# A hybrid attention, retention and MLP layer on one core: the MLP's weight sums move to the retention and through DRAM, and its blocks become one stream of loads

## The chip, the core and the metric

The kernel is one launch on one core of a Trainium2 chip. The metric is device time in microseconds; a kernel's time is the median of its runs. All arithmetic is float32. A matrix product is made in three TensorE passes over a high and a low part of each operand (type fp32r): high times high, high times low, low times high. The high part is a cast by ScalarE, the low part a subtraction by VectorE; together they are called a split here. TensorE is PE in the profile (PEld its weight loads), VectorE DVE, ScalarE ACT, GpSimd POOL, and SyncE SP; SP's queue issues every DMA.

## The reference

One layer over 1024 tokens of width 1024 with 256 context tokens. Cut to what matters here:

```python
# retention, 4 heads, chunks of 128 tokens, in two directions
out   = einsum(scores, vc) + einsum(qc, state) * xi
state = g_chunk * state + einsum(kc * zeta, vc)
...
x = x + g1 * _merge(o_na, o_ret, xga, xgb, w_proj_na[l], w_proj_ret[l], w_out[l])
hx2 = _modulate(_rmsnorm(x, norm2_g[l]), sh2, sc2)
x = x + g2 * _conv_ffn(hx2, w_up[l], conv_w[l], conv_b[l], w_down[l])

def _conv_ffn(h, w_up, conv_w, conv_b, w_down):
    u = h @ w_up                      # 1024 x 1024 by 1024 x 5632
    ...                               # depthwise convolution over 3 tokens
    a, val = jnp.split(u, 2, axis=-1)
    return (jax.nn.silu(a) * val) @ w_down   # 1024 x 2816 by 2816 x 1024
```

## The kernel before

The stages follow one another: modulation and first products, neighbourhood attention, retention, gates and projections, the output projection, then the MLP as an up product, a convolution and a down product. A planner in the framework sets the order of the instructions on every engine from the recorded program and its own costs; only the very end is written out by hand (`tc.manual_schedule()`). Each engine then works its list strictly in that order, and so does SP's queue: a transfer that waits for an engine holds back every transfer behind it.

**The MLP** makes its products by Strassen's scheme in Winograd's form: seven block products in place of eight, each of sums of blocks. With blocks A11, A12, A21, A22 the sums are S1 = A21 + A22, S2 = S1 - A11, S3 = A11 - A21, S4 = A12 - S2; on the other side T1 to T4 in the same way. There are 22 column blocks j of the up product (`NF`), in pairs of `NH` = 11. The first two are made plainly (`PLAIN`), the other 20 by `Unit7`. `Unit7.load` (L1544 to L1550) loads four 128x512 blocks of `w_up` and lets GpSimd make the four sums `s`; `prod` splits a block or a sum into `wc` and multiplies (L1590). Then `conv` makes a block of the activation; for the second block of a pair GpSimd makes the activation's own four sums `sa` (L1519), and all seven go to DRAM as `d_a`.

**The down product** has seven steps of 11 blocks (`steps`). For each block it loads an activation block from `d_a` (`ra`, split into `ahl`) and takes a weight block or a sum (split into `wc`), and makes 12 matmuls on four banks `y`. GpSimd makes the sums of `w_down` (`sub`, L1676) after the first and the second step in the program's order: for T1 the blocks come as `ur`, the sum is stored to DRAM as `d_w` (L1684) and loaded again for the fifth step; T2, T3 and T4 stay in SBUF tiles `T`.

**The retention** has four heads. A head's work comes in 14 slots: 10 of `front` (two chunks of context, eight of tokens: project a chunk to queries, keys and values) and four of `gate`. `slot` runs a slot's main work in three steps; between them it puts `turn` (the transposes `tp` of the chunk before), `mix` (the chunk outputs of the head before) and `state` (`kz`, `dS`). GpSimd has three small jobs there, each awaited by others: `r` (L1110), the end of the rotary embedding, from which PE makes `tp` and ScalarE and VectorE make `kz`; `SS` (L1170), the low part of the states, from which PE makes `Q`; and `mvr` (L1197), a power. The head's weights come as `raw<-in_w_ret` and `raw<-in_w_rg` in three buffers (L86).

Of the kernel before, what the change touches and what calls it, by code (L numbers as in the profile page):

```python
# [16 lines left out]
P = 128  # L17
D = 1024
KB = D // P
T = 1024  # L20
# [20 lines left out]
def tile_hybrid_layer(ctx, tc: tile.TileContext, io, dbg=None):  # L41
# [18 lines left out]
    d_w = dram.tile([NF // 2, P, 512], F32, name="d_w")  # L60
# [1169 lines left out]

    def slot(main, mix, head=None, i=None):
        def step():
            next(main, None)

# [45 lines left out]
    for _ in tl:  # L1280
        pass
# [201 lines left out]
    NH = NF // 2  # L1483
    A11, A12, A22, S1, S2, S3, S4 = range(7)

    def ur_tile(name):
        return rp.tile([P, 512], F32, tag="r", bufs=12, name=name)

    def ur_load(src, name="ur"):
        t = ur_tile(name)  # L1490
        sync.dma_start(t, src)
        return t

# [30 lines left out]
    def comb(c):  # L1524
        t = [tpl.tile([P, 4, KH, P], F32R, name=f"T{c}{i}") for i in range(2)]
        for b in range(4):
            raw = ur_load(d_t[c, b], "b")
            split(t[0][:, b], t[1][:, b], raw.rearrange("p (k t) -> p k t", k=KH))
# [11 lines left out]
    class Unit7:  # L1540
# [3 lines left out]
        def load(self):  # L1544
            self.a21, self.a22, self.a11, self.a12 = [ur_load(io["w_up"][self.j, b, i], "a") for b, i in ((1, 0), (1, 1), (0, 0), (0, 1))]
            self.s1, self.s2, self.s3, self.s4 = (ur_tile("s") for _ in range(4))
            pool.tensor_tensor(self.s1, self.a21, self.a22, ALU.add)
            pool.tensor_tensor(self.s2, self.s1, self.a11, ALU.subtract)
            pool.tensor_tensor(self.s3, self.a11, self.a21, ALU.subtract)
            pool.tensor_tensor(self.s4, self.a12, self.s2, ALU.subtract)  # L1550

        def prod(self, bank, a, c, first, last):
            w = wtile()
            split(w[:, 0], w[:, 1], a)
# [3 lines left out]
        def step(self, n):  # L1558
            if n == 0:
                self.load()  # L1560
# [5 lines left out]
                self.prod(self.X, self.a11, "B11", True, False)  # L1566
                act.copy(self.p1, self.X)  # L1567
            elif n == 1:
                self.prod(self.Y, self.s2, "T2", True, False)
                vec.tensor_tensor(self.u2, self.Y, self.p1, ALU.add)  # L1570
            elif n == 2:
                self.prod(self.Z, self.s1, "T1", True, False)
            elif n == 3:
                self.prod(self.Y, self.s3, "T3", False, False)
                vec.tensor_tensor(self.u3, self.Y, self.p1, ALU.add)  # L1575
                vec.tensor_tensor(self.value[:, 512:1024], self.Z, self.u3, ALU.add)
            elif n == 4:
                self.prod(self.X, self.a12, "B21", False, True)
                act.copy(self.gate[:, 0:512], self.X)
            elif n == 5:  # L1580
                self.prod(self.Y, self.a22, "T4", False, True)
                vec.tensor_tensor(self.value[:, 0:512], self.Y, self.p1, ALU.add)
            else:
                self.prod(self.Z, self.s4, "B22", False, True)
# [7 lines left out]
    seq = [j + NH * i for j in range(NH) for i in range(2)]  # L1592

    PLAIN = 2
# [11 lines left out]
    for _, i, n in sorted((7 * i + 2 * n, i, n) for i in range(PLAIN, NF) for n in range(7)):  # L1606
# [16 lines left out]
    wd = io["w_down"]  # L1623
# [235 lines left out]
```

## Time and profile before

| | us |
|---|---|
| runs | 1840.24, 1847.33, 1847.97; median 1847.33 |
| the profiled execution | 1837.61 |
| its span, first to last instruction | 1835.8 |
| PE busy in the span | 1758.8 |
| attention | 90 to 395 of the span |
| retention | 395 to 790 |
| gates and projections | 790 to 1040 |
| output projection | 1040 to 1157 |
| up product and convolution | 1157 to 1575 |
| down product | 1575 to the end |

The profile names a group by line, engine, operation and tiles (out<-in, buffer numbers left out). "Idle before" is the time in which the engine had nothing to run ahead of that group, and the arrow names what ended most of it. In a list of waits the last three fields are the total in us, the number of waits and the longest. Matmuls overlap: one of 128x512 is shown at some 390 ns, but one starts every 230 ns or so. A few matmul records are missing from the trace.

### The profile page before, as it was taken

The numbers are of one execution on the slowest core, as the hardware profiler recorded it, in microseconds if no ns is written. First come the engines' busy times: TensorE is split into PE (matmuls) and PEld (weight loads), VectorE is DVE, ScalarE is ACT, GpSimd is POOL, SyncE is SP. The second block draws the span as 40 slices with busy tenths as digits, with TensorE's granted clock in tenths as the row PEclk, the third lists the DMA queues.
The fourth block names the chain that finished last, engine by engine and source line by source line (L and its number), as shares of the span: only waits on it lengthen the run. The fifth ranks groups of instructions, "written<-read, shape, count | busy, mean of one in ns | idle before, by whom it ended". The sixth has DMA issues, their size and how long they took to land.

```text
span 1835.8 us, 24501 instructions
## 1 busy us (share of the span) xinstructions
PE 1758.8 (96%) x8477; PEld 1452.0 (79%) x8477; DVE 1217.0 (66%) x2386; ACT 824.0 (45%) x1768; POOL 517.7 (28%) x445
## 2 busy tenths in 40 slices
PE   8799999999999999999999999999999999938997
PEld 4588888888888888888888788788888888737886
DVE  5878887665666665631354657778888888635756
ACT  5666666553434342423422234544444444323544
POOL 2600000001212122210003400445554554356434
PEclk9799999999999999999999999999999999969999
DMA  9134344321212030323442435523323234688733
GB/s 353 46 112 133 95 121 144 117 83 35 69 33 81 17 99 16 92 86 111 148 127 62 137 138 187 190 75 121 109 89 113 87 102 134 233 308 275 251 119 145
DMA packets 121694, 229.10 MB, mean 125 GB/s; under 512 B 13888, under 2 KB 26336, under 8 KB 121568
## 3 DMA queue, kind: packets, MB, share of 16 engines
q1 hardware_dynamic: 121568, 227.52, 38.1%
q8 instruction: 67, 1.10, 0.3%
q14 instruction: 59, 0.48, 0.1%
HBM read 176.59 MB, written 48.25 MB: 122 GB/s over the span
## 4 chain that ended last, share of the span: by engine, by line
PE 76%; DMA 6%; POOL 5%; issue 5%; DVE 4%; ACT 2%; SPq 1%; POOLq 0%; ACTq 0%; DVEq 0%
PE u L1590 21%; PE mm L107 5%; PE mm L109 5%; PE mm L108 5%; PE mm L120 4%; PE mm L118 4%; PE mm L119 4%; DMA ur<-in_w_down 2%; PE R L506 2%; PE g L107 2%; PE g L108 2%; PE g L109 2%; PE om L118 2%; PE om L120 2%; PE ptp L488 2%
## 5 line engine op out<-in xcount | busy, mean ns | idle before, releaser
L1590 PE MATMUL y<-wc,ahl 128*128 128x512 f32 x924 | 215.7, 395 | 38.2 <-ACT ahl L81 31.3
L1590 PEld LDWEIGHTS y<-wc,ahl 128*128 128x128 f32 x924 | 175.9, 191 | 77.7 <-ACT ahl L81 31.7
L1590 PE MATMUL u<-T,wc 128*128 128x512 f32 x960 | 232.1, 396 | 3.4 <-ACT pu L1567 3.4
L1590 PEld LDWEIGHTS u<-T,wc 128*128 128x128 f32 x960 | 180.5, 188 | 48.4 <-ACT pu L1567 4.3
L108 PE MATMUL mm<-low,wc 128*128 128x512 f32 (+1 forms) x456 | 173.7, 381 | 0.0
L107 PE MATMUL mm<-hx,wc 128*128 128x512 f32 x392 | 158.1, 403 | 0.3 <-DVE vc L216 0.3
L109 PE MATMUL mm<-hx,wc 128*128 128x512 f32 x392 | 155.4, 396 | 0.0
L82 DVE TENSOR_TENSOR wc<-raw,wc 128x512 fp32r<-128x512 f32 x140 | 103.8, 745 | 55.1 <-ACT wc L81 54.7
L81 ACT CAST wc<-raw 128x512 fp32r<-128x512 f32 x140 | 86.8, 621 | 61.9 <-DMA raw<-in_w_gate 14.0
L1590 PE MATMUL u<-h2a,wc 128*128 128x512 f32 x480 | 112.8, 390 | 0.2 <-DVE pu L1575 0.2
L1590 PEld LDWEIGHTS u<-h2a,wc 128*128 128x128 f32 x480 | 90.0, 188 | 20.0 <-DVE pu L1575 0.6
L108 PEld LDWEIGHTS mm<-low,wc 128*128 128x128 f32 x456 | 86.0, 189 | 11.5
L81 ACT CAST wc<-s 128x512 fp32r<-128x512 f32 x80 | 49.6, 621 | 98.6 <-PE u L1590 91.6
L120 PE MATMUL mm<-wc,low 128*128 128x512 f32 (+1 forms) x240 | 91.5, 381 | 0.0
L109 PEld LDWEIGHTS mm<-hx,wc 128*128 128x128 f32 x392 | 73.7, 188 | 14.0
L82 DVE TENSOR_TENSOR wc<-s,wc 128x512 fp32r<-128x512 f32 x80 | 81.5, 1021 | 3.8 <-ACT wc L81 3.5
L107 PEld LDWEIGHTS mm<-hx,wc 128*128 128x128 f32 x392 | 73.9, 188 | 12.0 <-PE c L120 0.7
L82 DVE TENSOR_TENSOR ahl<-ra,ahl 128x512 fp32r<-128x512 f32 x77 | 65.3, 856 | 23.2 <-ACT ahl L81 23.2
L1325 POOL TENSOR_TENSOR col<-col,bcol 128x32 f32<-128x32 f32 x1 | 0.3, 256 | 282.3 <-DVE aw L533 282.3
L118 PE MATMUL mm<-wc,hx 128*128 128x512 f32 x192 | 75.3, 392 | 0.7 <-ACT r L1100 0.7
L119 PE MATMUL mm<-wc,hx 128*128 128x512 f32 x192 | 75.0, 390 | 0.0
L1110 POOL TENSOR_TENSOR r<-r,r 128x256 f32<-128x256 f32 x32 | 23.5, 735 | 172.1 <-DVE r L1109 160.0
(386 smaller groups left out, 4548.9 us busy)
## 6 DMA issues: line engine op xcount, KB each, us to landing
ur<-in_w_down SPq DMA_DIRECT2D x99, 256.0 KB, 3.9
a<-in_w_up SPq DMA_DIRECT2D x80, 256.0 KB, 2.8
ra<-d_a SPq DMA_DIRECT2D x77, 256.0 KB, 4.0
aw<-in_w_ada SPq DMA_DIRECT2D x32, 512.0 KB, 3.4
d_a<-sa SPq DMA_DIRECT2D x44, 256.0 KB, 2.0
d_a<-at SPq DMA_DIRECT2D x33, 256.0 KB, 2.7
x<-in_x SPq DMA_DIRECT2D x16, 512.0 KB, 6.2
raw<-in_w_gate SPq DMA_DIRECT2D x32, 256.0 KB, 2.9
```

The source lines that it names most:

```text
L81: act.copy(hi, src)
L82: (lo_eng or vec).tensor_tensor(lo, src, hi.bitcast(F32), ALU.subtract)
L107: pe.matmul(out, wh, xh, start=k == 0, stop=False)
L108: pe.matmul(out, wh, xl, start=False, stop=False)
L109: pe.matmul(out, wl, xh, start=False, stop=k == n - 1)
L118: pe.matmul(out, ah, bh, start=first, stop=False)
L119: pe.matmul(out, ah, bl, start=False, stop=False)
L120: pe.matmul(out, al, bh, start=False, stop=last)
L488: pe.transpose(tp[:, c], self.Pm[h][:, c * P : (c + 1) * P], ident)
L506: pe.matmul(R[:, h], self.pair.V[:, g, h].rearrange("p a b -> p (a b)"), self.PT[h][:, c].rearrange("p a b -> p (a b)"), start=c == 0, sto ...
L1110: pool.tensor_tensor(r0f, r0f, r1.rearrange("p q a t i -> p q (a t i)"), ALU.add)
L1590: pe.matmul(out, a, b, start=first and n == 0, stop=last and n == 2, skip_group_check=True)
```

## The change

GpSimd now makes the sums of `w_up` and of `w_down` during the retention. A generator `sums` has 31 jobs: 20 for the up blocks, 11 for pairs of down blocks. A job loads four 128x512 blocks into tiles `pj` (eight buffers, two jobs), makes four sums in place, and stores each to DRAM: S1 to S4 of block j in `d_s`, T1 to T4 in `d_w`. `slot` calls it once in each of its three steps, so that one sum is recorded per step; what is left at the end is done before the pools are released. In the MLP both products take their weight blocks and sums, and the down product its activations, from one `Stream`: a list of all loads in the order of use, six loads ahead of the block in use, in 12 buffers `ur`. `Unit7.load`, the sums of the down product and the 22 tiles `T` are gone. The number of matmuls is the same.

```diff
+    def sums():
+        jobs = []
+        for j in seq[PLAIN:]:
+            src = [io["w_up"][j, b, i] for b in range(2) for i in range(2)]
+            jobs.append((src, [(1, 2, 3, ALU.add, 3), (3, 0, 2, ALU.subtract, 2), (2, 3, 0, ALU.subtract, 0), (4, 1, 0, ALU.subtract, 1)], d_s[j]))
+        for j in range(NH):
+            src = [io["w_down"][dh, NH * i + j] for i in range(2) for dh in range(2)]
+            jobs.append((src, [(1, 1, 0, ALU.subtract, 0), (3, 3, 1, ALU.subtract, 1), (2, 3, 0, ALU.subtract, 3), (4, 2, 3, ALU.subtract, 2)], d_w[j]))
+
+        def load(job):
+            ts = [rt.tile([P, 512], F32, tag="pj", bufs=8, name="pj") for _ in range(4)]
+            for t, a in zip(ts, job[0]):
+                sync.dma_start(t, a)
+            return ts
+
+        todo, nxt = [], load(jobs[0])
+        for n, (_, ops, dst) in enumerate(jobs):
+            ts, nxt = nxt, load(jobs[n + 1]) if n + 1 < len(jobs) else None
+            for c, x, y, op, o in ops:
+                pool.tensor_tensor(ts[o], ts[x], ts[y], op)
+                while todo:
+                    sync.dma_start(*todo.pop())
+                todo.append((dst[c - 1], ts[o]))
+                yield
+        sync.dma_start(*todo.pop())
+
+    sums = sums()
...
         def step():
             next(main, None)
+            next(sums, None)
...
+    class Stream:
+        def get(self, src):
+            n = self.n
+            assert self.srcs[n] == src
+            for i in range(n, min(n + self.ahead + 1, len(self.srcs))):
+                if i not in self.tiles:
+                    self.tiles[i] = ur_load(source(*self.srcs[i]))
+            self.n += 1
+            return self.tiles[n]
...
-        def load(self):
-            self.a21, self.a22, self.a11, self.a12 = [ur_load(io["w_up"][self.j, b, i], "a") for b, i in ((1, 0), (1, 1), (0, 0), (0, 1))]
-            self.s1, self.s2, self.s3, self.s4 = (ur_tile("s") for _ in range(4))
-            pool.tensor_tensor(self.s1, self.a21, self.a22, ALU.add)
-            pool.tensor_tensor(self.s2, self.s1, self.a11, ALU.subtract)
-            pool.tensor_tensor(self.s3, self.a11, self.a21, ALU.subtract)
-            pool.tensor_tensor(self.s4, self.a12, self.s2, ALU.subtract)
...
-            split(w[:, 0], w[:, 1], a)
+            split(w[:, 0], w[:, 1], stream.get(("up", self.j, a)))
...
+    stream = Stream([("up", seq[i], UP[n]) for i, n in steps7] + [("down", j, c) for p in DOWN for j in range(NH) for c in p], 6)
...
+    def operands(p, j):
+        a, w = h2p.tile([P, 2, 512], F32R, tag="h2", bufs=KB, name="ahl"), wtile()
+        for t, c in zip((a, w), DOWN[p]):
+            split(t[:, 0], t[:, 1], stream.get(("down", j, c)))
+        return a, w
...
-    for j in range(NH):
-        t, b11, b22 = (ur_load(wd[x]) for x in ((1, j), (0, j), (1, NH + j)))
-        sub(t, t, b11)
-        sync.dma_start(d_w[j], t)
-        sub(T2[j], b22, t)
```

The planner places the new work. Three places matter to what follows.

First, GpSimd at the second head's fronts, where it also has the first head's mix. A row is a source line, an operation, and out<-in; the numbers belong to `r` and the first states. Before:

```order
L1110 TENSOR_TENSOR r_5537<-r_5537,r_5538 128x256
L1170 TENSOR_TENSOR SS<-init_4442,SS 128x256
L1170 TENSOR_TENSOR SS<-run,SS 128x256
L1197 TENSOR_TENSOR mvr<-mvr,mhalf 128x1
L1110 TENSOR_TENSOR r_5635<-r_5635,r_5636 128x256
L1170 TENSOR_TENSOR SS<-init_5310,SS 128x256
L1197 TENSOR_TENSOR mvr<-mvr,mhalf 128x1
L1110 TENSOR_TENSOR r_5731<-r_5731,r_5732 128x256
```

With the change, in the same place:

```order
L1111 TENSOR_TENSOR r_5749<-r_5749,r_5750 128x256
L1257 TENSOR_TENSOR pj<-pj 128x512 x4
L1171 TENSOR_TENSOR SS<-init_4443,SS 128x256
L1171 TENSOR_TENSOR SS<-run,SS 128x256
L1198 TENSOR_TENSOR mvr<-mvr,mhalf 128x1
L1257 TENSOR_TENSOR pj<-pj 128x512 x3
L1111 TENSOR_TENSOR r_5861<-r_5861,r_5862 128x256
L1257 TENSOR_TENSOR pj<-pj 128x512
L1171 TENSOR_TENSOR SS<-init_5490,SS 128x256
L1198 TENSOR_TENSOR mvr<-mvr,mhalf 128x1
L1257 TENSOR_TENSOR pj<-pj 128x512 x4
L1111 TENSOR_TENSOR r_5963<-r_5963,r_5964 128x256
```

Seven sums stand between the first `r` and the second, five between the second and the third. Counted over the whole list, the first head's fronts have eight sums ahead of the first `r` and four between any two; the gates after the first head have 20 and those after the second 23; the third head's fronts have five, seven, one and three, and all 124 stand ahead of its fifth `r`.

Second, SP's queue between the first head's fronts and its gates. Before, the loads of the gates' weights stood there alone:

```order
L1046 DMA rope<-in_rope 128x576
L1051 DMA dtab<-in_dtab 128x512
L86 DMA raw<-in_w_rg 128x512 x7
L86 DMA raw<-in_w_ret 128x512 x8
L1208 DMA d_oret<-ot 128x2x128
```

With the change, after the loads of nine jobs and the stores of seven:

```order
L1250 DMA pj<-in_w_up 128x512 x4
L1259 DMA d_s<-pj 128x512
L87 DMA raw<-in_w_rg 128x512
L1259 DMA d_s<-pj 128x512 x2
L1250 DMA pj<-in_w_up 128x512
L1259 DMA d_s<-pj 128x512
L1250 DMA pj<-in_w_up 128x512 x2
L87 DMA raw<-in_w_rg 128x512
L1250 DMA pj<-in_w_up 128x512
L87 DMA raw<-in_w_rg 128x512
L1259 DMA d_s<-pj 128x512 x3
L87 DMA raw<-in_w_rg 128x512
```

The loads of the gates' weights now stand behind stores that wait for GpSimd's sums.

Third, SP's queue at the down product, where the loads of the second step's activations (S2, from `d_a`) are. Before:

```order
L1684 DMA d_w<-ur 128x512
L1491 DMA ur<-in_w_down 128x512 x4
L1684 DMA d_w<-ur 128x512
L1491 DMA ur<-in_w_down 128x512
L1491 DMA ra<-d_a 128x512
L1684 DMA d_w<-ur 128x512
L1491 DMA ra<-d_a 128x512 x10
L1491 DMA ur<-in_w_down 128x512 x33
```

With the change:

```order
L1525 DMA ur<-in_w_down 128x512
L1525 DMA ur<-d_a 128x512
L1525 DMA ur<-d_w 128x512
L1525 DMA ur<-d_a 128x512
L1525 DMA ur<-d_w 128x512
L1687 DMA xr<-d_x_59 128x512
L1525 DMA ur<-d_a 128x512
L1525 DMA ur<-d_w 128x512
L1561 DMA d_a<-at 128x512
L1562 DMA d_a<-at 128x512
L1568 DMA d_a<-sa 128x512 x3
L1525 DMA ur<-d_a 128x512
```

The second step's loads no longer stand behind the stores of `d_w`. Three blocks of that step come ahead of the last pair's activation stores (`d_a<-at`, `d_a<-sa`), the rest behind them.

86 lines of the change are left out of this document (43 added, 43 removed).

## The prediction

> **What bounds the kernel now.** I read the head of the page first, then busy time by stage, then the list of waits of PE, and last the timelines around the longest waits.
>
> ```profile
> span 1835.8 us, 24501 instructions
> PE 1758.8 (96%) x8477; PEld 1452.0 (79%) x8477; DVE 1217.0 (66%) x2386; ACT 824.0 (45%) x1768; POOL 517.7 (28%) x445
> ```
>
> PE is busy all but 77 us. Nothing in the change alters its matmuls, so a gain can only come out of those 77 us, and every new wait of PE is a loss. By stage (columns: stretch, its length, busy us of PE, PEld, DVE, ACT, POOL, granted clock, DMA share, GB/s):
>
> ```profile
> 395.00:790.00 395.00, 394.14 (x2025) 336.06 (x2023) 240.37 (x757) 155.76 (x404) 84.68 (x123) 1.00 0.20 57
> 1186.00:1560.00 374.00, 374.00 (x1609) 302.11 (x1610) 318.75 (x328) 166.93 (x232) 195.18 (x113) 1.00 0.32 104
> 1610.00:1836.00 226.00, 185.41 (x792) 151.10 (x792) 130.94 (x165) 91.44 (x173) 111.08 (x96) 0.91 0.65 221
> ```
>
> The retention (first row) and the up product (second) leave PE no idle time at all; the down product (third) does. PE's waits there and at the start of the up product:
>
> ```profile
> PE y L1590 <- ACT ahl L81: 31.3, 1, 31.3
> PE y L1590 <- ACT wc L81: 4.2, 1, 4.2
> PE u L1590 <- ACT pu L1567: 3.4, 1, 3.4
> ```
>
> One wait holds most of it. PE's timeline puts it between the first and the second step of the down product:
>
> ```profile
> 1599.69 3.79 PE L1590 MATMUL y<-wc,ahl 128*128 128x512 f32 x16
> 1634.75 32.30 PE L1590 MATMUL y<-wc,ahl 128*128 128x512 f32 x132 [31.27 <-ACT ahl L81]
> 1671.26 0.80 PE L1590 MATMUL y<-wc,ahl 128*128 128x512 f32 x1 [4.20 <-ACT wc L81]
> 1673.01 111.14 PE L1590 MATMUL y<-wc,ahl 128*128 128x512 f32 x480 [0.96 <-DVE wc L82]
> ```
>
> What PE waits for is the split of an activation block. Its load (`ra`) stands on SP's queue behind the stores of `d_w`, and these wait for GpSimd's sums, which wait for their own loads:
>
> ```profile
> SPq L1684 <- POOL ur L1676: 27.5, 11, 5.5
> POOL T L1676 <- DMA ur<-in_w_down: 20.2, 6, 10.4
> ```
>
> **The change, part by part: the MLP.** Loads, sums and stores of this chain leave the down product, so the 31.3 us go. The two waits after it, for splits of `T`, go too: 4.2 + 1.0. After the long wait the 132 matmuls took 32.30 us, 244.7 ns each, where the later 480 took 231.5 ns each: 132 x 13.2 ns = 1.7 us more, which belong to the wait. I checked whether the next thing on the queue brings the stall back. Of the second step's loads, all but three blocks stand behind the last activation stores, whose sums GpSimd ended at 1594.2:
>
> ```profile
> 1592.95 1.29 POOL L1519 TENSOR_TENSOR sa<-at,sa 128x512 f32<-128x512 f32 x1
> ur<-in_w_down SPq DMA_DIRECT2D x99, 256.0 KB, 3.9
> d_a<-sa SPq DMA_DIRECT2D x44, 256.0 KB, 2.0
> ```
>
> A fourth block is thus there at about 1594.2 + 2.0 (its store) + 3.9 (a load) + 1.5 (two splits) = 1601.6; PE ends the first step at 1603.5 and has three blocks of 12 x 0.2315 = 2.8 us first. So 10 us are spare. A step wants two loads of 256 KB per 2.8 us, 190 GB/s, less than the 221 above. At the start of the up product the wait of 3.4 us stands behind GpSimd's first sums among other things; I take half, 1.7 (bounds 0 and 3.4). In the up product itself GpSimd's 80 sums and what they cost VectorE go, but PE was already at 374 of 374: nothing. Sum for the MLP: 31.3 + 4.2 + 1.0 + 1.7 + 1.7 = **39.9 us gained**.
>
> **The retention.** 124 sums, 124 loads and 124 stores come to a stage in which PE has 0.9 us of idle time. GpSimd alone had room there:
>
> ```profile
> 401.00:627.00 226.00, 225.88 (x1168) 193.30 (x1169) 139.33 (x455) 87.37 (x231) 47.72 (x70) 1.00 0.17 47
> 396.25 4.04 DMA dtab<-in_dtab
> 454.00:501.00 47.00, 47.00 (x249) 41.04 (x248) 30.41 (x85) 22.05 (x55) 13.03 (x19) 1.00 0.31 82
> 550.00:597.00 47.00, 47.00 (x249) 41.02 (x248) 30.32 (x85) 20.71 (x54) 13.00 (x19) 1.00 0.27 81
> ```
>
> The first row is the stretch into which the order puts the sums: from where their first loads can land (the load of `dtab`, second row, whose place they take, lands at 400.3) to the third head's fifth `r`. It has 226 us, 47.7 of them taken. What a sum of this size costs depends on what runs beside it (group of the tile `s` in the up product: count, then duration in ns, least/median/most):
>
> ```profile
> L1548 POOL TENSOR_TENSOR s<-s,a x20: 1267/1294/1728, 1174.0 to 1523.9; 128x512 f32<-128x512 f32 x20
> L1549 POOL TENSOR_TENSOR s<-a x20: 1293/2358/2364, 1175.7 to 1525.9; 128x512 f32<-128x512 f32 x20
> L1549 POOL TENSOR_TENSOR s<-a 128x512 f32<-128x512 f32 x20 | 44.4, 2220 | 10.7 <-DVE wc L82 10.7
> L1550 POOL TENSOR_TENSOR s<-a,s 128x512 f32<-128x512 f32 x20 | 41.5, 2077 | 1.5
> L1547 POOL TENSOR_TENSOR s<-a 128x512 f32<-128x512 f32 x20 | 31.3, 1566 | 124.6 <-DVE wc L82 76.0 <-DVE T L82 35.2 <-DMA a<-in_w_up 6.4
> L1548 POOL TENSOR_TENSOR s<-s,a 128x512 f32<-128x512 f32 x20 | 26.7, 1336 | 41.8 <-issue 28.2 <-DVE wc L82 13.4
> ```
>
> Undisturbed it is 1.28 us; over the four lines the mean is (44.4 + 41.5 + 31.3 + 26.7) / 80 = 1.80. VectorE is what disturbs it there, with operations that take two SBUF tiles. The rule is the Trainium skill's, page "SBUF — State Buffer", section "Who interferes with whom": such an operation and a GpSimd operation that reads SBUF lock each other out for a whole instruction. The trace agrees in kind (1.29 against 2.36 us on one line).
>
> The busiest of these groups of VectorE took 78.1 + 49.5 (splits) + four of about 30 + 23.0 (convolution), some 265 us or 71% of the up product's 374 (first two rows); in the retention they are the next three,
>
> ```profile
> L82 DVE TENSOR_TENSOR wc<-s,wc 128x512 fp32r<-128x512 f32 x77 | 78.1, 1015 | 3.2 <-ACT wc L81 2.9
> L1503 DVE SCALAR_TENSOR_TENSOR ta<-uu,cw,ta 128x1023 f32<-128x1023 f32 x18 | 30.5, 1693 | 0.0
> L82 DVE TENSOR_TENSOR wc<-raw,wc 128x512 fp32r<-128x512 f32 x58 | 44.5, 770 | 14.6 <-ACT wc L81 14.6
> L1129 DVE SCALAR_TENSOR_TENSOR kz<-r,dec,kz 128x128 fp32r<-128x128 f32 x80 | 27.1, 351 | 26.7 <-ACT kz L1128 26.3
> L1173 DVE SCALAR_TENSOR_TENSOR run<-run,dec,ds 128x256 f32<-128x256 f32 x24 | 11.6, 484 | 18.6 <-POOL SS L1170 18.5
> ```
>
> with `A` (8.8) and `wx` (5.3) 97 us of 395, 25%. Between 1.28 and 1.80 I take 1.28 + 0.52 x 25/71 = 1.46 us (bounds 1.28 and 1.80). Then 124 x 1.46 + 47.7 = 229 us of work stand in 226: GpSimd is just full, and wherever the order has more sums between two awaited jobs than fit, PE waits. The spare time of `r` comes from one slot:
>
> ```profile
> 428.21 0.73 POOL L1110 TENSOR_TENSOR r<-r,r 128x256 f32<-128x256 f32 x1 [5.70 <-DVE r L1109]
> 430.68 0.37 PEld L1118 LDWEIGHTS tp<-ident,r 128*128 128x128 f32 x2
> 434.64 0.73 POOL L1110 TENSOR_TENSOR r<-r,r 128x256 f32<-128x256 f32 x1 [5.70 <-DVE r L1109]
> 501.41 0.74 POOL L1110 TENSOR_TENSOR r<-r,r 128x256 f32<-128x256 f32 x1 [2.11 <-DVE r L1109]
> 508.98 0.74 POOL L1110 TENSOR_TENSOR r<-r,r 128x256 f32<-128x256 f32 x1 [2.44 <-DVE r L1109]
> 516.93 0.74 POOL L1110 TENSOR_TENSOR r<-r,r 128x256 f32<-128x256 f32 x1 [3.15 <-DVE r L1109]
> ```
>
> `r` ends at 428.94 and its transpose starts at 430.68: 1.74 us of slack. Slots are 6.43 us apart in the first head and 7.57 and 7.95 in the second. With 1.46 us a sum:
> - First head, eight sums ahead of the first `r`: 401 + 11.7 + 0.7 = 413.4 for an end that was at 409.6; less the slack, 2.0 lost. Then four sums and `r` are 6.57 in 6.43: 7 x 0.14 = 1.0.
> - Gates: 20 x 1.46 + 13.0 = 42 of 47, then 23 x 1.46 + 13.0 = 46.6 of 47.2: no loss, the slack comes back (0.6 of it the second time).
> - Second head: seven sums, two `SS` (0.74 each), `mvr` (0.55) and `r` are 13.0 in 7.57 + 1.74: 3.7. Five sums with one `SS` are 9.3 in 7.95: 1.4. The rest fits.
> - Third head: 10.1 in 7.57 + 0.6: 1.9; then seven sums, 12.2 in 7.9: 4.4.
>
> Sum 14.4 us; with 1.28 the same count gives 6.4, with 1.80 the stretch is full throughout and 124 x 1.80 + 47.7 - 226 - 1.7 = 43 us are lost. A gain is excluded: PE has nothing to gain there. SP: the gates' weights stand behind stores that wait for sums. They are late by at most a load, 3.9 us, at each of three gates; bounds 0 and 12, I take 3, nearer to 0, since they are asked for ahead of use. DMA: a job of eight transfers of 256 KB in 6.43 us is 326 GB/s, under what a stretch of the down product moved:
>
> ```profile
> 1635.00:1650.00 15.00, 15.00 (x58) 12.12 (x59) 11.69 (x15) 8.39 (x14) 4.76 (x4) 0.86 1.03 378
> ```
>
> VectorE is at 61% in the retention and at 85% in the up product without a wait of PE: nothing for what GpSimd costs it. **Retention: 17.4 us lost.**
>
> **The sum.** 1837.6 (the profiled execution) - 39.9 + 17.4 = 1815. The runs shown have a median 9.7 us above that execution; I add half of it: **1820 us**.
>
> **The rivals.**
> - *The sums are hidden.* GpSimd's 1.28 us holds, since VectorE's operations in the retention are short (351 ns against 1.3 us in the up product), and loads come in time: 1837.6 - 39.9 + 6.4, and 4.9 for the runs: 1809. Against it: two intervals with seven sums, which don't fit in any case.
> - *GpSimd becomes the bound of the retention,* the case on the other side. A sum and VectorE's operations with two SBUF tiles take turns, and PE, which follows GpSimd in every slot, goes at its pace; the weights of the gates wait behind the late stores. With 1.80 us a sum: 43 + 12 lost, 1837.6 - 39.9 + 55, and 4.9: 1858. It outweighs the MLP's gain from 124 x m + 47.7 - 226 - 1.7 + 12 = 39.9 on, that is m = 1.67 us. For it speaks that GpSimd is full at 1.46 already; against it the third of VectorE's load. Strict turns, by the skill's page named above, would be 124 x 1.28 + 47.7 + 25% of 226 = 263 us in 226: 37 lost in place of 14, and the whole at 1837 to 1849.
> - *The stall in the down product comes back in part,* because the stores of the last activations are later than at present and the second step's loads stand behind them. With half of the 31.3 us left: 1820 + 16 = 1836. Against it the 10 us of room worked out above.
>
> **How the numbers follow.** The forecast has 0.50, hidden sums 0.20, GpSimd as bound 0.17, the returning stall 0.08, 0.05 for others. Half a per cent, 9 us around 1847.3, is what a measurement can tell from no change: faster is below 1838. Of the forecast nearly all, of hidden sums all, of the returning stall more than half, of GpSimd as bound little lies there: 0.73 faster, 0.15 the same, 0.12 slower. The range from 1798 to 1846 holds the forecast with its bounds and the hidden sums and leaves out most of the case on the other side. The forecast's own range is 1804 to 1836.
>
> **What will show it.** Right: no wait of PE for `ahl` over 5 us, no `L1676` on GpSimd, PE's idle time in the down product under 6 us; in the retention PE idle 10 to 25 us, ended by `r`, `tp`, `kz` or `SS` behind `pj`, most at the second and third head's first fronts; `pj` at 1.4 to 1.5 us. Wrong: `pj` over 1.67 us or PE idle over 40 us in the retention; or waits for `raw<-in_w_rg` or for the loads of `pj` as the larger part of PE's new idle time, in which case SP and the transfers decide and not GpSimd's speed.

## The result, and the profile after

| | before | with the change |
|---|---|---|
| median of the runs | 1847.65 us | 1865.58 us |
| ratio | 1 | 1.0101, 95% interval 1.0069 to 1.0133 |
| span of the profiled execution | 1835.8 us | 1864.0 us |

The change makes the kernel slower by 1%; 1820 us, with a range from 1798 to 1846, was forecast. The profiled execution of the kernel before is 10 us faster than its median, so the spans differ by 28.2 us where the medians differ by 17.9. Three stretches show where the time went. They are cut at the first matmul of the gates (`g`) and at the first of the down product (`y`). The columns are the stretch, its length, busy us of PE, PEld, VectorE, ScalarE and GpSimd, the granted clock of TensorE, the DMA share and GB/s. First the kernel before:

```profile
395.00:809.50 414.50, 413.64 (x2120) 352.24 (x2119) 250.35 (x784) 160.82 (x415) 88.24 (x128) 1.00 0.20 58
809.50:1564.60 755.10, 747.50 (x3281) 608.18 (x3280) 511.01 (x671) 304.48 (x478) 257.75 (x158) 1.00 0.37 121
1564.60:1836.00 271.40, 224.10 (x961) 182.24 (x959) 157.83 (x196) 107.65 (x197) 129.77 (x108) 0.92 0.65 220
```

The same three with the change:

```profile
395.00:885.30 490.30, 438.32 (x2120) 364.53 (x2120) 294.10 (x784) 159.34 (x414) 253.10 (x252) 0.95 0.57 182
885.30:1635.10 749.80, 745.50 (x3280) 606.92 (x3279) 471.81 (x671) 305.14 (x478) 112.56 (x78) 1.00 0.44 142
1635.10:1864.00 228.90, 218.90 (x961) 179.67 (x959) 149.25 (x196) 106.37 (x197) 69.53 (x64) 0.99 0.63 211
```

The down product gains 42.3 us (before, the span ends at 1835.8, 0.2 us ahead of the cut) and what lies ahead of it 5.3, together 47.6. The retention loses 490.3 - 414.5 = 75.8 us. Of these, 51.1 are new idle time of PE (52.0 against 0.9). The other 24.7 are the same matmuls taking longer (438.3 us of busy time against 413.6), in a stretch whose granted clock is 0.95 and not 1.00. VectorE, too, is busy 44 us longer with the same 784 instructions, though the change gives it no work there. That was not forecast.

PE's waits within the retention, with the change (total us, number, longest):

```profile
PE tp L1119 <- POOL r L1111: 22.1, 9, 4.9
PE Ap L119 <- DVE ot L1207: 7.1, 2, 4.5
PE mm L120 <- DVE wc L83: 6.1, 4, 2.9
PE dS L121 <- DVE kz L1130: 5.7, 5, 2.8
PE Q L120 <- POOL SS L1171: 5.0, 2, 3.2
```

GpSimd's `r` and `SS` are the largest part, 27.1 us, as forecast. The rows for VectorE (`ot`, `wc`, `kz`) make 18.9; the prediction named only `kz` of these, and that as late behind `pj`. GpSimd's sums (count | busy us, mean ns | idle time before them and what ended it):

```profile
L1257 POOL TENSOR_TENSOR pj<-pj 128x512 f32<-128x512 f32 x124 | 165.2, 1333 | 72.1 <-DMA pj<-in_w_up 34.2 <-DMA pj<-in_w_down 20.4 <-DMA d_s<-pj 4.9
```

A sum takes 1.33 us, hardly more than undisturbed. So GpSimd is not slowed. It does wait for the sums' own loads, with `r` queued behind them. Two of VectorE's groups changed. Before:

```profile
L1198 DVE TENSOR_SCALAR o<-o,mvr 128x256 f32<-128x256 f32 x32 | 13.2, 414 | 19.7 <-POOL mvr L1197 19.7
```

With the change (`kz` was at 351 ns before, in the row quoted in the prediction):

```profile
L1130 DVE SCALAR_TENSOR_TENSOR kz<-r,dec,kz 128x128 fp32r<-128x128 f32 x80 | 41.5, 534 | 52.4 <-ACT kz L1129 52.2
L1199 DVE TENSOR_SCALAR o<-o,mvr 128x256 f32<-128x256 f32 x32 | 22.1, 690 | 36.8 <-POOL mvr L1198 36.8
```

And two stretches, one among the last sums and the one behind them:

```profile
655.00:675.00 20.00, 13.34 (x55) 10.35 (x54) 10.25 (x30) 3.13 (x10) 14.91 (x16) 0.83 0.60 198
705.00:885.00 180.00, 180.00 (x915) 152.48 (x914) 107.92 (x323) 70.19 (x175) 39.98 (x58) 1.00 0.24 68
```

In the slice where PE idles a third of the time the granted clock is 0.83; behind the sums PE is full again at 1.00. In kind this agrees with the Trainium skill, page "TensorE: Matmul & The Clock Gate", part 1, by which the clock is granted by how busy TensorE has lately been. The whole loss lies in the 310 us with sums.

### The profile page after: what moved, and what is told of

Its sections match the earlier page's. It is cut to its first block, busy times and chain, and to the rows that moved or that the text cites. A ratio compares the mean times of both kernels' runs of the same rounds, so it can differ in the third digit from the quotient of the medians.

```text
span 1864.0 us, 25043 instructions
## 1 busy us (share of the span) xinstructions
PE 1774.5 (95%) x8477; PEld 1457.9 (78%) x8477; DVE 1213.7 (65%) x2386; ACT 821.8 (44%) x1768; POOL 478.8 (26%) x445
## 4 chain that ended last, share of the span: by engine, by line
PE 71%; POOL 8%; issue 7%; DMA 7%; DVE 4%; ACT 2%; SPq 1%; POOLq 0%; ACTq 0%; DVEq 0%
PE u L1629 20%; PE mm L108 4%; PE mm L110 4%; PE mm L109 4%; PE y L1629 4%; POOL pj L1257 3%; DMA d_s<-pj 2%; PE mm L120 2%; PE R L507 2%; PE mm L121 2%; PE mm L119 2%; PE ptp L489 2%; PE g L110 2%; PE g L109 2%; PE g L108 2%
## 5 line engine op out<-in xcount | busy, mean ns | idle before, releaser
L82 ACT CAST wc<-ur 128x512 fp32r<-128x512 f32 x217 | 134.3, 620 | 231.4 <-PE u L1629 150.1
L83 DVE TENSOR_TENSOR wc<-ur,wc 128x512 fp32r<-128x512 f32 x217 | 172.2, 796 | 86.5 <-ACT wc L82 86.4
L1629 PE MATMUL y<-wc,ahl 128*128 128x512 f32 x924 | 210.4, 389 | 1.8 <-DVE wc L83 1.8
L1257 POOL TENSOR_TENSOR pj<-pj 128x512 f32<-128x512 f32 x124 | 165.2, 1333 | 72.1 <-DMA pj<-in_w_up 34.2
L83 DVE TENSOR_TENSOR wc<-raw,wc 128x512 fp32r<-128x512 f32 x140 | 109.3, 786 | 47.2 <-ACT wc L82 45.9
L1567 POOL TENSOR_TENSOR sa<-at 128x512 f32<-128x512 f32 x22 | 38.6, 1755 | 377.5 <-DVE at L1553 377.5
L1129 ACT ACTIVATE kz<-r,dec 128x128 fp32r<-128x128 f32 x80 | 30.2, 399 | 114.5 <-POOL r L1111 114.2
```

The costliest lines, as they stand in the source:

```text
L82: act.copy(hi, src)
L83: (lo_eng or vec).tensor_tensor(lo, src, hi.bitcast(F32), ALU.subtract)
L1257: pool.tensor_tensor(ts[o], ts[x], ts[y], op)
L1567: pool.tensor_tensor(prev[c], x, y, o)
L1629: pe.matmul(out, a, b, start=first and n == 0, stop=last and n == 2, skip_group_check=True)
```

## The experiments

Each run's loss is the length of its retention, from 395 to the first matmul of `g`, less the 414.5 us of the kernel before. Where the MLP is that of the change, what follows takes 978 to 981 us in all of them, so that the loss alone decides the time. A kernel that was run once has no interval; the kernel before had medians from 1840 to 1844 us beside these runs. Theories at the start: the loads and stores crowd or block SP's queue (A); GpSimd's sums stand in front of awaited jobs (B).

**Transfers without sums.** The sums alone are left out (the MLP multiplies unsummed blocks).

```diff
             for c, x, y, op, o in ops:
-                pool.tensor_tensor(ts[o], ts[x], ts[y], op)
```

> Leaves out the 124 sums on GpSimd; all loads of pj and all stores to d_s and d_w stay, so that the MLP multiplies unsummed blocks. Theory A, the loop of transfers (a load waits until the store from the same buffer has landed, and the loads and stores stand in SP's queue ahead of the retention's weights): the retention keeps more than half of its loss of 76 us, though nothing is left on GpSimd; 45 to 70 us over before, whole time 1835 to 1860. Theory B, GpSimd's time and the uneven order of its sums: the loss falls under 15 us, whole time 1800 to 1810.

1814.88 us, loss 25.4, between the two. The retention, and three slices of it:

```profile
395.00:834.90 439.90, 423.00 (x2117) 357.45 (x2117) 249.77 (x784) 160.31 (x413) 89.04 (x128) 0.98 0.62 203
415.00:435.00 20.00, 17.22 (x78) 14.11 (x77) 9.58 (x36) 6.76 (x21) 1.46 (x2) 0.91 0.90 302
555.00:575.00 20.00, 14.39 (x62) 11.81 (x61) 9.19 (x23) 7.66 (x19) 1.88 (x3) 0.83 0.96 305
635.00:655.00 20.00, 20.00 (x104) 16.83 (x103) 11.13 (x42) 5.11 (x15) 2.93 (x5) 1.00 0.96 322
```

In the first two slices the DMA engines are 90 and 96% busy at some 300 GB/s, and PE waits. In the third they are as busy, and PE is full: the share alone doesn't decide. Which awaited load stood behind which transfer was not traced. VectorE is back at 250 us. So transfers cost by themselves, and not all of the loss.

**Sums without transfers.** 124 sums on eight tiles that are filled once; no loads, no stores; the MLP loads plain blocks in place of sums.

```diff
-            ts, nxt = nxt, load(jobs[n + 1]) if n + 1 < len(jobs) else None
+            ts = sets[n % 2]
...
-                while todo:
-                    sync.dma_start(*todo.pop())
-                todo.append((dst[c - 1], ts[o]))
```

> Leaves out the loads of pj and the stores; the 124 sums stay in their place and work on eight tiles that are set to zero once. The MLP loads weight blocks in place of the sums, as many and in the same order. Theory A: the loss in the retention falls to what the uneven order costs, under 15 us, whole time 1795 to 1812. Theory B: it stays over 40 us, whole time 1830 or more. This run also has the price of the sums and of their exclusion with VectorE by itself.

1903.14 us, loss 113.3: more than the whole change. With no load to wait for, the planner packed the sums denser still, as GpSimd's timeline shows:

```profile
398.72 33.27 POOL L1254 TENSOR_TENSOR pj<-pj 128x512 f32<-128x512 f32 x26 [19.21 <-DVE pj L1250]
...
450.63 0.72 POOL L1111 TENSOR_TENSOR r<-r,r 128x256 f32<-128x256 f32 x1
451.31 18.37 POOL L1254 TENSOR_TENSOR pj<-pj 128x512 f32<-128x512 f32 x15
471.83 0.73 POOL L1111 TENSOR_TENSOR r<-r,r 128x256 f32<-128x256 f32 x1 [2.14 <-DVE r L1110]
```

Fifteen sums, 18.4 us, between two `r` whose slot had 6.43 us. The planner seems to reckon a sum at far less than it takes (its costs are not shown here). So this run says nothing of transfers; it shows that the order can cost more than they do.

**No stores.** Loads and sums as in the change; the stores are left out and the MLP loads plain blocks.

```diff
-                while todo:
-                    sync.dma_start(*todo.pop())
-                todo.append((dst[c - 1], ts[o]))
```

> Leaves out the 124 stores alone; loads and sums stay, the MLP loads weight blocks in place of the sums. Theory A in the form that the store's landing is what holds the next load: the loss in the retention falls to 10 to 25 us, whole time 1800 to 1820. Theory A in the form that the loads themselves are late (their number on the queue and their 3.7 us): 35 to 60 us of loss stay, 1830 to 1855. Theory B: the loss stays at 65 to 76 us.

1870.51 us, loss 81.1, with denser sums again (the last begins at 599 us of the span, with the change at 700). Leaving out the stores gains nothing; what they cost by themselves is not shown, since the order changed with them.

**Only the down sums.** 44 sums of the 11 down jobs in the retention; the up sums in the MLP as before, and the stream for the down product alone.

```diff
-        for j in seq[PLAIN:]:
-            src = [io["w_up"][j, b, i] for b in range(2) for i in range(2)]
-            jobs.append(...)
```

> Only the 11 jobs of the down product's sums move to the retention, 44 sums, at three per slot; the up product's sums are made in the MLP as before. The stream serves the down product alone. Theory A and B both: the loss in the retention is about 44/124 of 76 us, 27 us, and the down product keeps its gain of 42 us: 1847 - 42 + 27 = 1832. If the first head's fronts, where nothing else is on GpSimd, take most of it, the loss is under 15 us and the whole 1820.

1812.21 us, ratio 0.9838 (0.9819 to 0.9857). Loss 16.6, and the down product, at 228.7 us, keeps its whole gain. Of the change only this part pays; the 80 up sums bought 5 us in the MLP.

The planner's order had spoilt two runs. The framework can keep an instruction where it is recorded (`tc.keep_in_program_order`, `late` in the kernel). This gives the same 124 sums at a pace of choice.

**Three and two sums to a slot.** The change with its sums kept in place; then the first of a slot's three steps without a sum, so that they reach to the end of the retention.

```diff
-                pool.tensor_tensor(ts[o], ts[x], ts[y], op)
+                late(pool.tensor_tensor(ts[o], ts[x], ts[y], op))
```

> The change as it is, but each sum is kept where it is recorded: at most three between two awaited jobs of GpSimd, in place of four to eight; the same 124 sums, loads and stores, spread to the fourth head. Theory (the order: sums stand in front of r, SS, mvr and kz in larger numbers than fit, about 50 of the 75.8 us that the retention lost, on top of some 25 for the transfers): three sums of 1.3 us and r are 4.6 us in a slot of 6.4, so r is not late; the retention loses about 25 us, the whole comes to 1815 to 1820, PE's waits for r and SS fall from 27 us to under 8. Rival (what 124 sums cost GpSimd and VectorE, whatever their order): the loss stays above 60 us, the whole above 1850. Rival (stores and loads on SP's queue are the larger part): sums of a job are further apart, the waits of SP for sums grow, the loss is 40 to 75.

> As the run before, but two sums to a slot, so that the 124 sums, loads and stores lie over the whole of the retention (about 390 us in place of some 300). Theory (order, and transfers that crowd the queue in dense stretches): two sums and r are 3.3 us in 6.4; loss 10 to 20 us, the whole 1800 to 1812. Rival (each sum with its transfers costs a fixed amount): as the run before within 4 us. Rival (the loads of the weights stand behind stores whatever the pace): 25 us or more lost, 1815 or later.

Three: 1849.99 us, ratio 1.0040 (1.0021 to 1.0060), loss 58.2. Two: 1830.14 us, ratio 0.9922 (0.9894 to 0.9951), loss 41.0. The order made 17.6 us of the 75.8, not 50; PE's waits for `r` did fall, to 5.4 and 4.3 us. Both losses lie where the rivals had them that blame the transfers on SP's queue; the narrow sums and the fills at two to a slot, further down, decide on that. At two to a slot there is room on GpSimd and on the queue, and 41 us remain. VectorE points to why (the retention row, then durations of `kz` and `o`: least/median/most, then PE's longest waits):

```profile
395.00:850.50 455.50, 429.28 (x2111) 357.59 (x2109) 334.39 (x782) 156.43 (x414) 255.28 (x252) 0.98 0.60 194
L1130 DVE SCALAR_TENSOR_TENSOR kz<-r,dec,kz x80: 335/924/1451, 398.5 to 785.1; 128x128 fp32r<-128x128 f32 x80
L1199 DVE TENSOR_SCALAR o<-o,mvr x32: 1343/1371/1379, 479.8 to 848.8; 128x256 f32<-128x256 f32 x32
PE mm L120 <- DVE wc L83: 9.1, 6, 2.4
PE Ap L120 <- DVE qk L1122: 4.8, 4, 1.2
PE tp L1119 <- POOL r L1111: 4.3, 4, 2.2
PE dS L121 <- DVE kz L1130: 3.4, 4, 0.8
```

VectorE is busy 334 us in place of 250. All 32 `o<-o,mvr` take 1.34 to 1.38 us and not 0.41. Of PE's 26.2 us of idle time 19.5 end with VectorE, 9.1 of these with splits of weights (`wc`), which take 1.01 us on average and not 0.77. The two timelines at one place, GpSimd's and then VectorE's, show what they wait for:

```profile
647.26 0.72 POOL L1111 TENSOR_TENSOR r<-r,r 128x256 f32<-128x256 f32 x1 [2.21 <-DVE r L1110]
647.94 2.58 POOL L1257 TENSOR_TENSOR pj<-pj 128x512 f32<-128x512 f32 x2
...
648.45 2.22 DVE L1130 SCALAR_TENSOR_TENSOR kz<-r,dec,kz 128x128 fp32r<-128x128 f32 x2 [0.95 <-ACT kz L1129]
```

GpSimd ends `r` and starts two sums, until 650.52. Half a microsecond later VectorE's two `kz`, which need that `r`, start; they take 2.22 us in place of some 0.7 and end at 650.67, with the sums. Who starts first holds the other: here the sums, since they follow at once on the very `r` or `mvr` from which VectorE's operation is made. Theory C: GpSimd's reads hold VectorE.

**Narrow sums.** The change with sums over 64 of the 512 columns, in nearly its order, at 0.32 us.

```diff
-                pool.tensor_tensor(ts[o], ts[x], ts[y], op)
+                pool.tensor_tensor(ts[o][:, :64], ts[x][:, :64], ts[y][:, :64], op)
```

> The change with sums over 64 of the 512 columns (the products of the sums are then wrong in the other columns, which takes no time away from them): nearly the same order, the same number of instructions, loads, stores and waits, but a sum of about 0.2 us. Theory (GpSimd's time in front of awaited jobs makes some 50 us, transfers some 25): loss about 25 us, 1815. Rival (the chain of load, sum, store and the next load into the same buffer delays the queue, whatever a sum takes): loss over 50 us, above 1840.

1829.36 us, loss 39.3, just between the theories. VectorE is at 249.5 us. That is 14 us more than the loads and stores alone (25.4): here sums wait for the loads, with `r` behind them. The other 36.5 of the change's 75.8 come with the sums' length: time and reads together.

**Down sums in the gates.** The 44 sums recorded in the gates' chains, tiles from that stage's pool, the retention as before.

```diff
-                mm_a(m, wg, hxs(0, half), hxs(1, half))
+                for _ in chain(m, wg, hxs(0, half), hxs(1, half), 2):
+                    next(sums, None)
```

> Only the 44 sums of the down product are made ahead, and in the stage of the gates, where no other engine waits for GpSimd; the up product's sums stay in the up product as before. Theory: the retention is that of the kernel before (no loss), the down product keeps its gain of about 43 us, the gates' stage loses under 5 us: 1800 to 1806. Rival (the transfers cost wherever PE is full): the gates' stage loses 10 us or more, 1812 or later.

1820.62 us, ratio 0.987 (0.9837 to 0.9903). The retention lost 0.8 us, but the stretch from `g` to `y` grew by 23.8, as the rival had it. Two attempts to mend it follow: d_ona's blocks loaded ahead into buffers of their own, and then a slower pace (four buffers, each job's loads after the job before).

```diff
+    on = [ona_load(n) for n in range(KB)]
...
-            raw = rawload(d_onat[n * P : (n + 1) * P])
+            raw = on[n]
```

> The 44 down sums in the stage of the gates, with the blocks of d_ona loaded into five buffers of their own ahead of the sums' loads. In the run before, PE waited 15.2 us there for three of these blocks behind the loads and stores of the sums. Theory: that wait goes and the clock with it, the gates cost under 8 us in place of 24: 1800 to 1808. Rival (the queue is full there, and the weights of the gates are late in place of d_ona): waits for wc behind raw<-in_w_gate of 8 us or more, 1812 to 1820.

> The 44 down sums in the stage of the gates with four buffers in place of eight, each job's loads only after the stores of the job before, and all eight d_ona blocks ahead. In the two runs before the queue carried about 300 GB/s at a DMA share of 0.9 for 80 us and the blocks of d_ona or the gates' weights came 15 us late. Theory (density of the transfers): at half the pace the share stays under 0.6 and the weights are in time; the gates lose under 8 us: 1800 to 1808. Rival (the weights' loads stand behind stores that wait for sums): waits for wc of 8 us or more remain, 1810 to 1825.

1818.60 us, ratio 0.9859 (0.9819 to 0.9898), and 1832.08 us, ratio 0.9938 (0.9914 to 0.9961). PE's largest new wait in the three, in this order (`tpn` are the transposes of d_ona's blocks, `pn` the first projection behind the gates):

```profile
PE tpn L1354 <- DMA raw<-d_ona: 15.2, 3, 10.5
PE g L108 <- ACT wc L82: 16.2, 2, 9.1
PE pn L108 <- ACT wc L82: 25.7, 1, 25.7
```

What is moved ahead on the queue makes the next thing late: first d_ona, then the gates' weights. Half the pace was meant, but the 44 sums took 115 us in place of 86, at a DMA share of 0.76; they last into the projection and hold up its weights. Both times it was the rival, that weights stand behind the sums' transfers, and at the slower pace it went beyond the rival's time too.

**Reads taken away.** Each sum is replaced by three constant fills of its result tile, of about its length; loads, stores and pace stay. First at three to a slot; beside it, three sums to a slot on resident tiles with no transfers.

```diff
-                late(pool.tensor_tensor(ts[o], ts[x], ts[y], op))
+                for w in (512, 512, 320):
+                    late(pool.memset(ts[o][:, :w], 0.01))
```

> The kernel with three sums to a slot, each sum replaced by three constant fills of its result tile (512, 512 and 320 columns, together about as long as a sum, by the fill of 1280 columns that took 1.18 us; the products of these sums are then wrong). GpSimd's time, order, loads, stores and waits are nearly those of three sums to a slot; what is gone is that GpSimd reads SBUF. Theory (VectorE's operations with two SBUF tiles are held for a whole sum, and PE waits for VectorE): VectorE's busy time in the retention falls from 325 us back to about 250, kz to 0.35 us, o<-o,mvr to 0.41, and the loss of 58 us to 25 to 35 (transfers and their waits): 1815 to 1825. Rival (GpSimd's time in front of awaited jobs is the cause): the loss stays at 50 or more, 1840 or later.

> Three sums to a slot, kept where they are recorded, on tiles that stay in SBUF: no loads and no stores in the retention; the MLP multiplies plain blocks in place of the sums. Theory (loss of 58 us = 25 for transfers and some 33 for the sums themselves, through VectorE and GpSimd): loss 25 to 40, 1815 to 1830. Rival (the sums cost only where they wait for loads and the weights stand behind stores): loss under 12, below 1805. Against the unpaced sums alone (113 us lost) it also shows what the order makes.

Fills: 1828.44 us, loss 36.3, VectorE at 253 us. Sums alone: 1833.16 us, loss 43.0, VectorE at 334 us. So 22 us of the 58.2 go when fills stand in for the sums. Without any transfers the sums lose 43, somewhat more than the theory's 40; paced, they lose 70 us less than in the planner's order. The 36.3 left with the fills are larger than expected: PE still waits 14.1 us for `r`, and GpSimd waits 36.1 us for loads of `w_up`.

**One down sum to a slot, and narrow sums at two.** The first is the 44 down sums kept in place, one to a slot.

```diff
-            next(sums, None)
-
+
+        next(sums, None)
         step()
```

> The 44 down sums in the retention, one to a slot and kept where they are recorded, in place of the 85 us into which the planner packed them when only they were moved (16.6 us lost there). Theory (density of the transfers and sums in front of awaited jobs): DMA share about 0.35, one sum between two r; what is left is VectorE held by the sums' reads, 44/124 of 22 us: loss 5 to 10 us, 1800 to 1807. Rival (each sum with its transfers costs a fixed 0.4 us): loss 15 us or more, 1810 or later.

> 124 sums over 64 of 512 columns, two to a slot, kept where recorded; all loads and stores, spread over the whole retention (products of the sums wrong). Narrow sums in the planner's order lost 39 us, full sums at two to a slot 41. Theory (transfers cost by their density): spread over 400 us in place of 260 the queue has room, loss under 12 us: about 1800. Rival (124 loads and stores cost some 25 us whatever their density, since weights stand behind stores): loss 25 us or more, 1813 or later.

The down sums: 1804.26 us, ratio 0.9792 (0.9768 to 0.9817), loss 7.9. It beats both kernels and is the fastest version that makes whole sums. Narrow sums at two: 1794.72 us, loss 5.3, with all 124 loads and stores. Their retention:

```profile
395.00:814.80 419.80, 416.26 (x2121) 351.77 (x2119) 249.45 (x784) 158.35 (x414) 135.68 (x252) 1.00 0.65 211
```

The same transfers that lost 39.3 us in the planner's order lose 5.3 over 400 us. So 124 loads and stores need not cost 25 us; their density and the order of the sums that wait for them changed together, and which of the two counts is not shown. That leaves 36 us between narrow and full sums at the same pace: GpSimd's time, or its reads.

**Fills at two to a slot.** The fills of before, at two to a slot.

> Two sums to a slot over the whole retention, each replaced by three constant fills of its result (512, 512 and 320 columns, together 1.42 us before, a sum 1.39 us; the products of the sums are wrong). Loads, stores, GpSimd's time and order stay near those of full sums at two to a slot (41.0 us lost); GpSimd only writes SBUF. Narrow sums at the same pace lost 5.3 us. Theory (what full sums add is VectorE, held for a whole sum where an operation of it wants a second SBUF tile): kz at 0.35 us, loss 5 to 12 us, 1793 to 1801. Rival (GpSimd's time, in front of r, SS and mvr): loss 25 us or more, 1813 or later; between them both have a part.

1791.85 us, loss 2.0.

```profile
395.00:811.50 416.50, 414.40 (x2124) 352.69 (x2123) 255.20 (x785) 160.17 (x416) 253.95 (x496) 1.00 0.65 213
L1130 DVE SCALAR_TENSOR_TENSOR kz<-r,dec,kz x80: 337/351/354, 401.1 to 746.5; 128x128 fp32r<-128x128 f32 x80
L1258 POOL MEMSET pj<- 128x512 f32 (+1 forms) x368 | 170.1, 476 | 36.4 <-DMA pj<-in_w_up 24.4 <-DMA pj<-in_w_down 0.2
```

GpSimd is busy 254 us, as with the sums (255), the transfers are the same, and next to nothing is lost. (The 36.3 us with fills at three to a slot were thus a matter of pace, and GpSimd waited 12 us longer for loads there, 36.1 against 24.4.) So at this pace neither GpSimd's time (theory B) nor the transfers (A) make the loss: 39 of the 41 us come from how full sums hold VectorE. By the Trainium skill, page "SBUF — State Buffer", section "Who interferes with whom", a VectorE instruction with two SBUF inputs contends with a GpSimd instruction that reads SBUF, not with one that only writes. `kz` agrees: 0.92 us beside sums, 0.35 beside fills.

`o<-o,mvr`, with one SBUF tile and two per-partition scalars, does not fit that reading. Its durations beside fills, and one meeting, GpSimd's row first:

```profile
L1199 DVE TENSOR_SCALAR o<-o,mvr x32: 579/583/587, 473.1 to 810.4; 128x256 f32<-128x256 f32 x32
500.10 1.56 POOL L1258 MEMSET pj<- 128x512 f32 x3
500.19 0.58 DVE L1199 TENSOR_SCALAR o<-o,mvr 128x256 f32<-128x256 f32 x1 [0.95 <-POOL mvr L1198]
```

A fill of 512 columns takes 0.53 us, and `o` ends 0.14 us behind it, as it ends 0.15 us behind a sum (begun at 643.75 us with full sums). So a fill seems to hold it as a sum does, only for a shorter time. The fills took away two things at once, the reads and the length of a GpSimd instruction, and how the 39 us divide between them is open: sums cut into three were not run.

**Sums behind kz.** If the cost hung on the operation that follows a sum's start, it would go when the sums start after it. A one-column GpSimd operation that reads `kz` was put ahead of each pair of sums; in a second version `kz` was recorded in the slot of its own `r`.

```diff
+            late(pool.tensor_scalar(junk, kz[:, 1, 1, :1].bitcast(F32), 1.0, None, ALU.add))
+        next(sums, None)
+        next(sums, None)
```

> All 124 sums, two to a slot as in the run that lost 41.0 us, but each pair stands behind a one-column GpSimd operation that reads the kz just made, so that the sums start when VectorE has ended kz and not in the moment before. Theory (a sum that starts just before kz holds it for its whole length, and PE's dS and the slot behind it): kz back to about 0.35 us, the loss falls from 41 to 10 to 20 us: 1800 to 1810; what is left is o<-o,mvr, the splits wc, and two sums that now end close to the next r. Rival (VectorE has to wait somewhere, whichever operation it meets): loss 35 us or more, 1823 or later.

> As the run before, whose one-column operation read the kz of the chunk before, which was long made, so that the sums started where they had before. Now it reads the kz of the r that has just ended: kz is recorded in the slot of its r, and in the fronts the two sums start behind it. Theory (the cost is tied to the operation that follows each sum's start): GpSimd waits about 1.5 us in front of the one-column operation, kz is at 0.35 us in the fronts, loss 10 to 25 us in place of 41 and 50: 1800 to 1815. Rival (VectorE meets the reads somewhere in any case, or the later sums now delay the next r): loss 35 us or more, with waits for r or VectorE's busy time still above 320 us.

First version: 1840.77 us, ratio 0.9993 (0.9977 to 1.0010), loss 49.7. The edit missed its aim. The `kz` it read was that of the chunk before, so GpSimd hardly waited and the sums met the same `kz`:

```profile
L1285 POOL TENSOR_SCALAR jk<-kz 128x1 f32<-128x1 f32 x40 | 11.6, 290 | 1.2 <-DVE kz L1130 1.2
```

Second version: 1838.88 us, ratio 0.9975 (0.9959 to 0.9992), loss 51.8. Here GpSimd's waits, `kz` and PE's waits were:

```profile
DVE kz L1131: 73.6, 33
L1131 DVE SCALAR_TENSOR_TENSOR kz<-r,dec,kz x80: 339/351/354, 400.5 to 793.6; 128x128 fp32r<-128x128 f32 x80
PE mm L120 <- DVE wc L83: 8.6, 6, 2.4
PE Q L120 <- POOL SS L1176: 8.0, 7, 1.7
PE tp L1121 <- POOL r L1113: 6.7, 4, 3.0
L83 DVE TENSOR_TENSOR A<-A,A 128x128 fp32r<-128x128 f32 x32 | 24.2, 755 | 11.7 <-ACT A L82 11.7
```

`kz` is free of the sums and VectorE's busy time falls from 334 to 289 us, yet the loss is 51.8 and not 41.0. GpSimd now idles 73.6 us ahead of the sums, `SS` and `r` are awaited for longer (14.7 us against 4.3), and the sums meet other VectorE operations (the split of `A` at 755 ns, 293 before). So it isn't one meeting that can be dodged by moving the sums within a slot. Which of PE's waits each meeting causes stays open.

## Why the prediction was wrong

**The losses by run**, in us of retention, for what each kernel adds to it:

| | planner's order | three to a slot | two to a slot |
|---|---|---|---|
| 124 full sums, loads, stores | 75.8 | 58.2 | 41.0 |
| sums replaced by fills | not run | 36.3 | 2.0 |
| sums of 64 columns | 39.3 | not run | 5.3 |
| loads and stores alone | 25.4 | not run | not run |
| sums alone | 113.3 | 43.0 | not run |

- **The MLP** was right in kind and a little small: 47.6 us gained, 39.9 forecast. The stall went, with no long wait in its place. The up product with its start, put at 1.7, gained 5.5 (383.6 to 378.1 us).
- **The retention** failed: 75.8 us lost, 17.4 forecast. Four of its steps did, two of them terms put at nothing.
- *"VectorE is at 61% in the retention ...: nothing for what GpSimd costs it."* By the fills, what full sums do to VectorE costs 22 us at three to a slot and 39 at two. The prediction knew that the two engines lock each other out, but charged the lock to GpSimd alone: 1.46 us a sum. It was 1.33. The one to wait is VectorE, whose short operations come just after a sum has begun; in the up product, whose rows set the price, GpSimd had been the one to wait (2.36 us). VectorE's busy share was the wrong measure: its operations are steps of a chain on which PE waits, so a held one can count whatever the mean load. In the change's own order this term was not measured by itself. It is a part of the 36.5 us that full sums add to narrow ones, and PE's waits there name `r` and `SS` first.
- *"DMA: ... 326 GB/s, under what a stretch of the down product moved"*, so nothing. It left out the stretch's own traffic, 47 to 82 GB/s by the rows quoted, which makes 373 to 408, about or over the 378. Transfers alone lost 25.4 us, with stretches at 0.9 of the DMA engines' time and some 300 GB/s. *SP's late weights* (3 us, at most 12) may be a part of this; how large a part is open.
- *The count of intervals*, 14.4 us by 1.46 us a sum, left out that sums wait for their loads with `r` behind them, and took only the uneven places as lost. Kept in place, with three between two `r`, the change still loses 58.2; the planner's unevenness makes 17.6. The term's own size is near this, in part by luck: it was summed with 1.46 us a sum and without any wait for loads.
- *Idle time was taken as the whole loss.* A third of it, 24.7 us, is the same work at a lower clock. The prediction had seen this in the down product (1.7 us behind the long wait) and not asked it of its own new waits.
- **The rivals.** GpSimd as the bound had the right side and nearly the time (1858), but by luck: it was to decide from 1.67 us a sum, and the sums stayed at 1.33. The turns named there do occur, but mostly at VectorE's cost. The returning stall did not occur. Of the signs of being wrong, PE idle over 40 us in the retention came (52.0), `pj` over 1.67 us did not.

What stays open: how the 36.5 us that full sums add to narrow ones in the planner's order divide into held VectorE operations and GpSimd's time (no fills were run in that order), how far the reads and how far the length of a sum make the hold, and how much of the fills' 36.3 at three to a slot is transfers and how much the length of GpSimd's work behind late loads.

## What to carry to other kernels

An engine that is idle isn't free to use: before work is moved to GpSimd, list which VectorE operations on the critical chain read two SBUF tiles, or follow a GpSimd result at once, and price each that can meet the new work at a whole GpSimd instruction. Price added transfers together with the traffic that is there, over the time into which the order packs them. Then look at the gain by parts: here 44 of the 124 sums brought some 42 of the 48 us, and spread at one to a slot they cost 8 and made the kernel 2.1% faster than before.

## What the runs showed of the hardware

- At two to a slot, GpSimd sums of 1.29 us held VectorE operations that started within them to their end (`o<-o,mvr` 1.37 us against 0.41, in all 32 cases; `kz` a median of 0.92 against 0.35), and most of the sums lost nothing (median 1.294 us against 1.28 undisturbed, mean 1.39).
- `o<-o,mvr`, with one SBUF tile and two per-partition scalars, was held by fills too, which read nothing: 0.58 us in all 32 cases, at a fill's 0.53. `kz` was not (0.34 to 0.35 us in all 80).
- TensorE's granted clock was 0.83 in a slice with a third of idle time, and over the retention, at 0.95, the same 2120 matmuls were 6% longer busy.
